# Decay logits of each head in 384 columns instead of 512, in a two-layer mLSTM and FoX trunk on one core

## The chip, the core and the metric

One core of a Trainium2 chip runs the whole program. Its engines work side by side and wait for each other by semaphores: TensorE (PE) multiplies matrices into PSUM, VectorE (DVE) and ScalarE (ACT) work on elements, GpSimd (POOL) does small jobs, SyncE (SP) issues most transfers from HBM. The metric is the device time of one execution in microseconds; the median of the runs of a kernel is compared.

## The reference

The input is 256 tokens of width 2048. Layer 0 mixes them by a stabilised mLSTM with 4 heads (queries and keys 256 wide, values 512), layer 1 by softmax attention with a forget gate (FoX, 16 heads of 128). Both are followed by a SwiGLU FFN of width 5632, and every norm is modulated by a condition vector (adaLN). Per head, the decayed scores of FoX are

```python
s = jnp.einsum('bhqd,bhkd->bhqk', qi, kf) * scale + cqi[..., None] - cum[..., None, :]
s = jnp.where(kpos[None, :] <= qpos[:, None], s, -jnp.inf)
p = jax.nn.softmax(s, axis=-1)
```

and those of the mLSTM

```python
D = b[..., :, None] - b[..., None, :] + lic[..., None, :]
D = jnp.where(causal, D, -jnp.inf)
m_t = jnp.maximum(inter_log, jnp.max(D, axis=-1))
w_intra = jnp.exp(D - m_t[..., None])
s = jnp.einsum('bhtd,bhsd->bhts', qc, kc) * w_intra
```

With two blocks of 128 tokens, the first block of queries sees only the first block of keys, the second sees both. So of 2 x 256 logits for each of 128 rows, 128 + 256 are used.

## The kernel before, in words

Nearly all the work is projections of the 256 tokens by weights that come from HBM in tiles of 1 MB. `fetch` (L252 to L255) loads such a tile into `rawp`, a pool of five buffers. `split` (L257) makes a high half (`hi`, a cast on ScalarE, L263) and a low half (`lo`, a subtraction on VectorE, L264) of each two rows of it, each from a pool of four buffers (`splitp`). `mm_t` (L287) then does three matmuls per piece: activation high by weight high (L290), high by low (L291), low by high (L292), 512 columns each. Their sums stand in six PSUM banks (`psum`, names mm); two more banks (`aux`) serve everything else: transposes, logits, scores.

The 1 MB tiles of the adaLN weights come through the same five buffers. `ada_tile` (L191) loads one on SyncE (L194) and multiplies and sums it on VectorE (L195, 128x2048). They are background work: a counter decides in which stage they are issued.

The mLSTM heads (`mlstm_head`) go in steps: `scores` (logits L678 and L683, exp L906, q·k L914, weighting L921), `flip` (transposes L893), `mix` (weights by values L945, squares L949, root L953, normalisation of both token blocks L957), `emit`. `emit` transposes the head into an aux bank (L970) and writes it scaled, as high half on ScalarE (L978) and low half on VectorE (L979), into a tile of `slots`; two such tiles a head. The steps of a head are laid between the matmuls of the stage that runs. Heads 2 and 3 fall into the beginning of the output projection (names mm_499, mm_500), which reads what `emit` wrote: its activations are first the slots of heads 0 and 1, then slot_493 and slot_495 of head 2. ScalarE's functions come from tables; exp, sigmoid (L800) and sqrt are in different ones, and a row ACT_TABLE_LOAD changes them.

`bridge` (L527) leads from one projection to the next through residual and norm. In its last part TensorE, VectorE and ScalarE follow the order in which the code is written: the last matmuls of the old projection for token block 0; on VectorE the gated residual (L429, L430); `rstd` (ScalarE's square and root, L457); `scale` (L474); transposes (L485); `high` (L495 on ScalarE, L497 on VectorE, four each); `low` (L510), the low half of the new activations; `begin` on TensorE, whose matmuls L552 and L553 need the high half and L556 the low half. Then the same again for token block 1. adaLN tiles that are still due are put between these rows when the program is built.

`split3` (L631) makes the decay sums of all heads of a layer into one tile `u3`: three bf16 parts at rows 0, 32 and 64. `logits` (L676) spreads the row of one head over 128 partitions by a matmul with a selecting column (`sel`, L678), and adds the causal mask of the diagonal blocks by another one (L683). In what order each engine takes its instructions is settled when the program is built, by a scheduler that models each instruction's time, except where the code fixes it.

Of the kernel before, what the change touches and what calls it, by code (L numbers as in the profile page):

```python
# [11 lines left out]
BF16 = mybir.dt.bfloat16  # L12
# [5 lines left out]
P = 128  # L18
T = 256
# [12 lines left out]
def kernel(  # L32
# [5 lines left out]
    nc = tc.nc  # L38
# [6 lines left out]
    att = ctx.enter_context(tc.tile_pool(name="att", bufs=1))  # L45
# [6 lines left out]
    def nm(s):  # L52
        n_name[0] += 1
        return f"{s}_{n_name[0]}"
# [21 lines left out]
    identb = const.tile([P, P], BF16, name="identb")  # L76
# [52 lines left out]
    for i, row in enumerate((crow, crow2)):  # L129
        for j in range(2):  # L130
            ps = bank()
# [497 lines left out]
        return u  # L629

    def split3(u, n, new):  # L631
        u3 = att.tile([96, T], BF16, tag="u3", name=nm("u3"), bufs=1)
        nc.gpsimd.memset(u3, 0.0)
        r = new()
        pp = new().bitcast(BF16)
        p, p2 = pp[:, :T], pp[:, T:]
        nc.vector.tensor_copy(p, u)
        nc.scalar.copy(u3[0:n, :], p)
        nc.vector.tensor_tensor(r, u, p, op=ALU.subtract)
        nc.vector.tensor_copy(p2, r)  # L640
        nc.scalar.copy(u3[32 : 32 + n, :], p2)
        nc.vector.tensor_tensor(r, r, p2, op=ALU.subtract)
        nc.scalar.copy(u3[64 : 64 + n, :], r)
        return u3

    def gate_weights(raw, pieces):
# [25 lines left out]
        nc.vector.tensor_tensor(g, ps[:n, :T], b, op=ALU.add)  # L672
        return g

    causal = ((0, P), (T, 2 * T))

    def logits(u3, h, ps, stop):
        nc.tensor.matmul(  # L678
            ps.rearrange("p (t s) -> p t s", t=2), sel[:, h : h + 1].to_broadcast([96, P]),
            u3[:, None, :].to_broadcast([96, 2, T]),  # L680
            start=True, stop=False, skip_group_check=True,
        )
        nc.tensor.matmul(  # L683
            ps.rearrange("p (b s) -> p b s", b=4)[:, 0::3, :], identb,
            mask[:, None, :].to_broadcast([P, 2, P]),
            start=False, stop=stop, skip_group_check=True,
        )
# [208 lines left out]
    def mlstm_head(hd, q, k):  # L896
        st = {}

        def scores():
            U = abank()  # L900
            logits(u3, hd, U, True)
            buf = slot()
            W = buf[:, : 3 * P]
            st["W"], st["WT"] = W, buf[:, 512 : 512 + 3 * P]
            for t in range(2):
                nc.scalar.activation(  # L906
                    W[:, slice(*packed[t])], U[:, slice(*causal[t])], AF.Exp,
                    bias=negT[:, t, hd : hd + 1],
                )
            S = abank()  # L910
            for t in range(2):
                n = P * (t + 1)
                for j in range(2):
                    nc.tensor.matmul(  # L914
                        S[:, T * t : T * t + n], q[:, j, t * P : (t + 1) * P], k[:, j, :n],
                        start=j == 0, stop=j == 1, skip_group_check=True,
                    )
            den = small([P, 2], "den", bufs=4)
            for t in range(2):
                wt = W[:, slice(*packed[t])]  # L920
                nc.vector.scalar_tensor_tensor(  # L921
                    out=wt, in0=S[:, slice(*causal[t])], scalar=1.0 / 16.0,
                    in1=wt, op0=ALU.mult, op1=ALU.mult, accum_out=den[:, t : t + 1],
                )
            r = small([P, 2], "r", bufs=4)
            nc.vector.scalar_tensor_tensor(
                out=r, in0=den, scalar=-1.0, in1=den, op0=ALU.mult, op1=ALU.max
            )
            nc.vector.tensor_tensor(r, r, em[:, :, hd], op=ALU.max)
            nc.vector.reciprocal(r, r)  # L930
            st["r"] = r
# [204 lines left out]
    def fox_head(hd, q, k):  # L1136
        st = {}

        def scores():
            S = abank()  # L1140
            logits(u3, hd, S, False)
            for t in range(2):
                n = P * (t + 1)
                nc.tensor.matmul(  # L1144
                    S[:, T * t : T * t + n], q[:, t * P : (t + 1) * P], k[:, :n],
                    start=False, stop=t == 1, skip_group_check=True,
                )
            mx = small([P, 2], "den", bufs=4)
            buf = slot()
            W = buf[:, : 3 * P]  # L1150
            st["W"], st["WT"] = W, buf[:, 512 : 512 + 3 * P]
            sm = small([P, 2], "r", bufs=4)
            for t in range(2):
                nc.vector.tensor_reduce(
                    out=mx[:, t : t + 1], in_=S[:, slice(*causal[t])], axis=AX.X, op=ALU.max,
                    negate=True,
                )
            for t in range(2):
                nc.scalar.activation(
                    W[:, slice(*packed[t])], S[:, slice(*causal[t])], AF.Exp,  # L1160
                    bias=mx[:, t : t + 1], accum_out=sm[:, t : t + 1],
                )
            nc.vector.reciprocal(sm, sm)
            for t in range(2):
                wt = W[:, slice(*packed[t])]
                nc.vector.tensor_scalar(wt, wt, sm[:, t : t + 1], None, op0=ALU.mult)
# [171 lines left out]
```

## Time and profile before

| | us |
|---|---|
| median of 3 runs | 2300.04 (2299.62 to 2301.35) |
| profiled execution | 2300.83 |
| its span | 2299.0 |
| TensorE busy | 2275.4 (99%) |
| VectorE busy | 1612.9 (70%) |
| ScalarE busy | 1122.8 (49%) |
| GpSimd busy | 15.6 (1%) |

The profiled execution is one run; its span is the time from the first to the last instruction in the profile, 1.8 us less than the run's own time. Busy times add up what an engine's instructions took. The granted clock of TensorE was 0.999 of full speed on average. The start-to-start distance of two matmuls tells what one costs in a row of them; its own duration is longer, since they overlap.

### The profile page before, as it was taken

The numbers are of one execution on the slowest core, as the hardware profiler recorded it, in microseconds if no ns is written. First come the engines' busy times: TensorE is split into PE (matmuls) and PEld (weight loads), VectorE is DVE, ScalarE is ACT, GpSimd is POOL, SyncE is SP. The second block draws the span as 40 slices with busy tenths as digits, with TensorE's granted clock in tenths as the row PEclk, the third lists the DMA queues.
The fourth block names the chain that finished last, engine by engine and source line by source line (L and its number), as shares of the span: only waits on it lengthen the run. The fifth ranks groups of instructions, "written<-read, shape, count | busy, mean of one in ns | idle before, by whom it ended". The sixth has DMA issues, their size and how long they took to land.

```text
span 2299.0 us, 26543 instructions
## 1 busy us (share of the span) xinstructions
PE 2275.4 (99%) x10376; PEld 1861.0 (81%) x10376; DVE 1612.9 (70%) x1829; ACT 1122.8 (49%) x1488; POOL 15.6 (1%) x40
## 2 busy tenths in 40 slices
PE   8999999999999999999999999999999999999998
PEld 4777878888888888888878888888888888888886
DVE  5998788878887878865687777777655554544554
ACT  3778664555543344444555444455444433444443
POOL 0000000000000000000000000000000000000000
PEclk9999999999999999999999999999999999999999
DMA  9998989798989889985667878775766555555552
GB/s 348 364 368 320 355 313 362 271 345 325 331 331 336 323 337 337 342 293 188 215 243 285 300 259 288 255 275 186 250 241 222 191 191 198 189 187 195 193 196 105
DMA packets 89090, 623.92 MB, mean 271 GB/s; under 512 B 10034, under 2 KB 10482, under 8 KB 14596
## 3 DMA queue, kind: packets, MB, share of 16 engines
q1 hardware_dynamic: 87552, 617.79, 74.3%
q0 software_dynamic: 1264, 4.29, 0.5%
q8 instruction: 81, 1.33, 0.2%
q14 instruction: 45, 0.37, 0.0%
q10 hardware_dynamic: 148, 0.14, 0.0%
HBM read 620.05 MB, written 2.13 MB: 271 GB/s over the span
## 4 chain that ended last, share of the span: by engine, by line
PE 88%; DVE 6%; DMA 3%; ACT 2%; issue 1%; SPq 0%; ACTq 0%; DVEq 0%
PE mm L292 25%; PE mm L291 25%; PE mm L290 25%; PE mm L273 5%; DVE ada L195 3%; PE mm L276 2%; DVE lo L264 2%; DMA ada<-in_ada_w_dram 2%; PE aux L347 1%; ACT hi L263 1%; DMA raw<-in_w_in_dram 1%; DMA slot<-in_w_in_dram 1%; PE aux L945 0%; PE aux L485 0%; PE aux L1144 0%
## 5 line engine op out<-in xcount | busy, mean ns | idle before, releaser
L264 DVE TENSOR_TENSOR lo<-raw,hi 128x1024 fp32r<-128x1024 f32 x764 | 926.9, 1223 | 556.8 <-ACT hi L263 556.2
L263 ACT CAST hi<-raw 128x1024 fp32r<-128x1024 f32 x764 | 797.1, 1053 | 920.3 <-PE mm L292 816.9
L291 PE MATMUL mm<-lo,hT 128*128 128x512 f32 x1840 | 718.3, 390 | 5.3 <-DVE lo L264 5.3
L290 PE MATMUL mm<-hi,hT 128*128 128x512 f32 x1840 | 719.3, 393 | 0.0
L292 PE MATMUL mm<-hi,hT 128*128 128x512 f32 x1840 | 718.1, 390 | 0.0
L195 DVE SCALAR_TENSOR_TENSOR ada<-ada,cs 128x2048 f32<-128x2048 f32 x192 | 438.9, 2286 | 49.2 <-DMA ada<-in_ada_w_dram 49.2
L291 PEld LDWEIGHTS mm<-lo,hT 128*128 128x128 f32 x1840 | 345.7, 188 | 80.1 <-DVE lo L264 10.2
L292 PEld LDWEIGHTS mm<-hi,hT 128*128 128x128 f32 x1840 | 345.4, 188 | 72.7 <-issue 0.5
L290 PEld LDWEIGHTS mm<-hi,hT 128*128 128x128 f32 x1840 | 345.3, 188 | 70.9 <-ACT hi L263 0.5
L290 PE MATMUL mm<-hi,slot 128*128 128x512 f32 x960 | 375.1, 391 | 0.2 <-ACT slot L978 0.2
L291 PE MATMUL mm<-lo,slot 128*128 128x512 f32 x960 | 374.4, 390 | 0.0
L292 PE MATMUL mm<-hi,slot 128*128 128x512 f32 x960 | 374.4, 391 | 0.0
L290 PEld LDWEIGHTS mm<-hi,slot 128*128 128x128 f32 x960 | 180.3, 188 | 37.7 <-ACT slot L978 0.8
L292 PEld LDWEIGHTS mm<-hi,slot 128*128 128x128 f32 x960 | 180.2, 188 | 37.6 <-issue 0.7
L291 PEld LDWEIGHTS mm<-lo,slot 128*128 128x128 f32 x960 | 180.2, 188 | 37.0
L273 PE MATMUL mm<-hT,hi 128*128 128x512 f32 x512 | 181.7, 402 | 0.6 <-DVE slot L359 0.6
L276 PE MATMUL mm<-hT,lo 128*128 128x256 f32 x512 | 138.3, 280 | 0.0
L273 PEld LDWEIGHTS mm<-hT,hi 128*128 128x128 f32 x512 | 94.4, 188 | 20.5 <-DVE slot L359 0.9
L276 PEld LDWEIGHTS mm<-hT,lo 128*128 128x128 f32 x512 | 96.6, 189 | 3.0
L800 ACT ACTIVATE slot<-mm 128x512 f32<-128x512 f32 x78 | 45.0, 593 | 33.9 <-PE mm L292 31.1
L435 ACT ACTIVATE t<-X 128x512 f32<-128x512 f32 x32 | 20.2, 631 | 39.2 <-DVE X L430 39.2
L1085 ACT ACTIVATE slot<-mm 128x512 f32<-128x512 f32 x44 | 25.4, 598 | 15.0 <-PE mm L292 13.8
(207 smaller groups left out, 980.5 us busy)
## 6 DMA issues: line engine op xcount, KB each, us to landing
ada<-in_ada_w_dram SPq DMA_DIRECT2D x192, 1024.0 KB, 6.5
raw<-in_gate_up_dram SPq DMA_DIRECT2D x176, 1024.0 KB, 4.9
raw<-in_down_dram SPq DMA_DIRECT2D x88, 1024.0 KB, 4.9
raw<-in_fox_in_dram SPq DMA_DIRECT2D x48, 1024.0 KB, 5.0
raw<-in_w_in_dram SPq DMA_DIRECT2D x44, 1024.0 KB, 7.3
raw<-in_w_out_dram SPq DMA_DIRECT2D x16, 1024.0 KB, 5.8
raw<-in_fox_out_dram SPq DMA_DIRECT2D x16, 1024.0 KB, 4.9
slot<-in_w_in_dram SPq DMA_DIRECT2D x16, 256.0 KB, 12.1
```

What stands on the lines that cost most here:

```text
L195: nc.vector.scalar_tensor_tensor(out=raw, in0=raw, scalar=1.0, in1=cs, op0=ALU.mult, op1=ALU.mult, accum_out=acc[layer][:, j : j + 1],)
L263: nc.scalar.copy(hi, raw[:, j : j + 2, :])
L264: nc.vector.tensor_tensor(lo, raw[:, j : j + 2, :], hi.bitcast(F32), op=ALU.subtract)
L273: nc.tensor.matmul(ps, hi, rhs, start=first, stop=last, skip_group_check=True)
L276: nc.tensor.matmul(ps[:, T:], lo, rhs[:, :T], start=False, stop=False, skip_group_check=True)
L290: nc.tensor.matmul(ps, a, hi, start=first, stop=False, skip_group_check=True)
L291: nc.tensor.matmul(ps, a, lo, start=False, stop=False, skip_group_check=True)
L292: nc.tensor.matmul(ps, b, hi, start=False, stop=last, skip_group_check=True)
L347: nc.tensor.transpose(ps[:, j * T + t * P : j * T + (t + 1) * P], src[:, t, (2 * i + j) * P : (2 * i + j + 1) * P], ident,)
L435: nc.scalar.activation(t512(), X[:, t, 512 * i : 512 * (i + 1)], AF.Square, accum_out=self.ss[:, t, i : i + 1],)
L800: nc.scalar.activation(SP[i][:, t, :], banks[t], func)
L1085: nc.scalar.activation(sg[:, t, :], banks[t], AF.Silu)
```

## The change

The causal pieces of the logits are put behind one another: the second block of queries, which sees all 256 tokens, in columns 0 to 255 of the bank, since the table now reads `causal = ((T, T + P), (0, T))`, so the first block's 128 columns stand at 256 to 383. `u3` gets 128 more columns that hold a copy of its first 128 (one more copy on ScalarE per layer, a wider memset on GpSimd). The selection matmul then writes 384 columns in one go instead of twice the 256; the mask matmul writes the two diagonal blocks, which are now neighbours, in columns 128 to 383; and the q·k matmuls of both kinds of head write where `causal` says. What reads the logits uses `causal` and follows.

```diff
-        u3 = att.tile([96, T], BF16, tag="u3", name=nm("u3"), bufs=1)
+        u3 = att.tile([96, T + P], BF16, tag="u3", name=nm("u3"), bufs=1)
         nc.gpsimd.memset(u3, 0.0)
...
-        nc.scalar.copy(u3[0:n, :], p)
+        nc.scalar.copy(u3[0:n, :T], p)
...
-        nc.scalar.copy(u3[32 : 32 + n, :], p2)
+        nc.scalar.copy(u3[32 : 32 + n, :T], p2)
...
-        nc.scalar.copy(u3[64 : 64 + n, :], r)
+        nc.scalar.copy(u3[64 : 64 + n, :T], r)
+        nc.scalar.copy(u3[:, T:], u3[:, :P])
         return u3
...
-    causal = ((0, P), (T, 2 * T))
+    causal = ((T, T + P), (0, T))

     def logits(u3, h, ps, stop):
         nc.tensor.matmul(
-            ps.rearrange("p (t s) -> p t s", t=2), sel[:, h : h + 1].to_broadcast([96, P]),
-            u3[:, None, :].to_broadcast([96, 2, T]),
+            ps[:, : T + P], sel[:, h : h + 1].to_broadcast([96, P]), u3,
             start=True, stop=False, skip_group_check=True,
         )
         nc.tensor.matmul(
-            ps.rearrange("p (b s) -> p b s", b=4)[:, 0::3, :], identb,
+            ps[:, P : T + P].rearrange("p (b s) -> p b s", b=2), identb,
             mask[:, None, :].to_broadcast([P, 2, P]),
...
-                        S[:, T * t : T * t + n], q[:, j, t * P : (t + 1) * P], k[:, j, :n],
+                        S[:, slice(*causal[t])], q[:, j, t * P : (t + 1) * P], k[:, j, :n],
...
-                    S[:, T * t : T * t + n], q[:, t * P : (t + 1) * P], k[:, :n],
+                    S[:, slice(*causal[t])], q[:, t * P : (t + 1) * P], k[:, :n],
```

With the new sizes the scheduler puts rows into another order in three stretches: where the mLSTM heads 2 and 3 meet the output projection, in the bridge to the first FFN, and by some exchanges in that FFN. In the FoX layer only the sizes change. Lines 645 to 681 stand one line lower in the changed kernel; from 682 on the numbers are the same in both. Of a name such as hi_532_2775 the middle number is the same in both kernels, and the last is higher by one in the changed one.

**ScalarE, head 2 into slot_493 and slot_495.** Before:

```order
L953 ACT_TABLE_LOAD
L953 ACTIVATE hrs_479_2530<-hsq_478_2529,eps_t_93 128x2
L263 CAST hi_525_2735<-raw_522_2729 128x1024
L402 COPY t512_483_2545<-aux_482_2543 16x128
L263 CAST hi_530_2771<-raw_529_2769 128x1024
L978 ACTIVATE slot_493_2590<-aux_494_2591,prm_115 128x256
L978 ACTIVATE slot_495_2600<-aux_496_2601,prm_115 128x256
L263 CAST hi_532_2775<-raw_529_2769 128x1024
L978 ACTIVATE slot_493_2590<-aux_494_2591,prm_115 128x256
L978 ACTIVATE slot_495_2600<-aux_496_2601,prm_115 128x256
```

Now:

```order
L263 CAST hi_525_2736<-raw_522_2730 128x1024
L953 ACT_TABLE_LOAD
L953 ACTIVATE hrs_479_2531<-hsq_478_2530,eps_t_93 128x2
L263 CAST hi_530_2772<-raw_529_2770 128x1024
L402 COPY t512_483_2546<-aux_482_2544 16x128
L263 CAST hi_532_2776<-raw_529_2770 128x1024
L978 ACTIVATE slot_493_2591<-aux_494_2592,prm_115 128x256
L978 ACTIVATE slot_495_2601<-aux_496_2602,prm_115 128x256
L978 ACTIVATE slot_493_2591<-aux_494_2592,prm_115 128x256
L978 ACTIVATE slot_495_2601<-aux_496_2602,prm_115 128x256
```

The root of head 2 (hrs_479) goes behind the cast of hi_525, and the cast of hi_532 ahead of the first two L978. A table load for the root stands in both; two more, not shown, stand ahead of these rows, where the exps of heads 2 and 3 now have a sigmoid between them (19 table loads in all before, 21 now).

**VectorE, the same stage.** Before:

```order
L957 SCALAR_TENSOR_TENSOR slot_477_2528<-aux_481_2534,hrs_479_2530,slot_104_541 128x512
L264 TENSOR_TENSOR lo_526_2736<-raw_522_2729,hi_525_2735 128x1024
L195 SCALAR_TENSOR_TENSOR ada_534_2803,acc0_124<-ada_534_2803,cs_144 128x2048
L264 TENSOR_TENSOR lo_531_2772<-raw_529_2769,hi_530_2771 128x1024
L979 SCALAR_TENSOR_TENSOR slot_493_2590<-aux_494_2591,prm_115,slot_493_2590 128x256
L979 SCALAR_TENSOR_TENSOR slot_495_2600<-aux_496_2601,prm_115,slot_495_2600 128x256
L264 TENSOR_TENSOR lo_533_2776<-raw_529_2769,hi_532_2775 128x1024
L979 SCALAR_TENSOR_TENSOR slot_493_2590<-aux_494_2591,prm_115,slot_493_2590 128x256
L979 SCALAR_TENSOR_TENSOR slot_495_2600<-aux_496_2601,prm_115,slot_495_2600 128x256
L195 SCALAR_TENSOR_TENSOR ada_546_2852,acc0_124<-ada_546_2852,cs_144 128x2048
```

Now:

```order
L957 SCALAR_TENSOR_TENSOR slot_477_2529<-aux_481_2535,hrs_479_2531,slot_104_541 128x512
L264 TENSOR_TENSOR lo_531_2773<-raw_529_2770,hi_530_2772 128x1024
L195 SCALAR_TENSOR_TENSOR ada_534_2804,acc0_124<-ada_534_2804,cs_144 128x2048
L264 TENSOR_TENSOR lo_533_2777<-raw_529_2770,hi_532_2776 128x1024
L979 SCALAR_TENSOR_TENSOR slot_493_2591<-aux_494_2592,prm_115,slot_493_2591 128x256
L979 SCALAR_TENSOR_TENSOR slot_495_2601<-aux_496_2602,prm_115,slot_495_2601 128x256
L195 SCALAR_TENSOR_TENSOR ada_546_2853,acc0_124<-ada_546_2853,cs_144 128x2048
L979 SCALAR_TENSOR_TENSOR slot_493_2591<-aux_494_2592,prm_115,slot_493_2591 128x256
L979 SCALAR_TENSOR_TENSOR slot_495_2601<-aux_496_2602,prm_115,slot_495_2601 128x256
```

The subtraction of lo_526 went ahead of this piece, that of lo_531 ahead of ada_534, that of lo_533 ahead of the first pair of L979, and ada_546 between the two pairs. On TensorE, fifteen matmuls of hi_513 and hi_515 stood between the transposes of head 2 (L970, aux_496) and the first matmul of hi_523 by slot_493; now there are two, and thirteen stand ahead of the transposes.

**VectorE, first half of the bridge and the beginning of the second.** Before:

```order
L429 TENSOR_TENSOR t512_639_3290<-mm_600_3143,slot_486_2550 128x512
L430 TENSOR_TENSOR X_129<-X_129,t512_639_3290 128x512
L457 RECIPROCAL rstd1_641_3316<-rstd1_641_3316 128x1
L474 TENSOR_SCALAR slot_642_3319<-X_129,rstd1_641_3316 128x512
L195 SCALAR_TENSOR_TENSOR ada_672_3526,acc0_124<-ada_672_3526,cs_144 128x2048
L497 TENSOR_SCALAR t512_645_3331<-aux_644_3326,mods0_122 128x128 x4
L510 TENSOR_TENSOR hT_134<-t512_645_3331,hT_134 128x4x128
L429 TENSOR_TENSOR t512_646_3356<-mm_601_3144,slot_486_2550 128x512
L430 TENSOR_TENSOR X_129<-X_129,t512_646_3356 128x512
L195 SCALAR_TENSOR_TENSOR ada_679_3566,acc0_124<-ada_679_3566,cs_144 128x2048
L457 RECIPROCAL rstd1_648_3361<-rstd1_648_3361 128x1
L474 TENSOR_SCALAR slot_649_3364<-X_129,rstd1_648_3361 128x512
```

Now:

```order
L429 TENSOR_TENSOR t512_639_3291<-mm_600_3144,slot_486_2551 128x512
L195 SCALAR_TENSOR_TENSOR ada_672_3527,acc0_124<-ada_672_3527,cs_144 128x2048
L430 TENSOR_TENSOR X_129<-X_129,t512_639_3291 128x512
L457 RECIPROCAL rstd1_641_3317<-rstd1_641_3317 128x1
L474 TENSOR_SCALAR slot_642_3320<-X_129,rstd1_641_3317 128x512
L497 TENSOR_SCALAR t512_645_3332<-aux_644_3327,mods0_122 128x128 x4
L195 SCALAR_TENSOR_TENSOR ada_679_3567,acc0_124<-ada_679_3567,cs_144 128x2048
L510 TENSOR_TENSOR hT_134<-t512_645_3332,hT_134 128x4x128
L429 TENSOR_TENSOR t512_646_3357<-mm_601_3145,slot_486_2551 128x512
L430 TENSOR_TENSOR X_129<-X_129,t512_646_3357 128x512
L457 RECIPROCAL rstd1_648_3362<-rstd1_648_3362 128x1
L474 TENSOR_SCALAR slot_649_3365<-X_129,rstd1_648_3362 128x512
```

ada_672 went from behind L474 to ahead of L430, and ada_679 from behind the second L430 to ahead of the first L510. In the second half, ada_686 now stands directly behind this piece, ahead of the four L497 and L510 of token block 1; before, those two followed with nothing between them. TensorE's rows of the bridge keep their order; on ScalarE some casts ahead of the first L429 changed places.

## Rows read from the trace of the kernel before

**Rows 1.** The page, busy us of each engine (share), and instructions.

```profile
PE 2275.4 (99%) x10376; PEld 1861.0 (81%) x10376; DVE 1612.9 (70%) x1829; ACT 1122.8 (49%) x1488; POOL 15.6 (1%) x40
```

**Rows 2.** TensorE's waits behind 445 us, the longest: total, times, longest us.

```profile
PE mm L556 <- DVE hT L510: 0.9, 1, 0.9
```

**Rows 3.** Timeline of TensorE, 276 to 279 us: start us, duration us, instruction.

```profile
276.57 0.39 PE L678 MATMUL aux<-u,sel 96*128 96x512 bf16 x1
276.80 0.27 PE L683 MATMUL aux<-mask,identb 128*128 128x256 bf16 x1
276.92 1.47 PE L914 MATMUL aux<-slot,slot 128*128 128x128 f32 x8
```

**Rows 4.** Timeline of ScalarE, 300 to 345 us.

```profile
324.53 1.28 ACT L906 ACT_TABLE_LOAD   x1
325.82 0.73 ACT L906 ACTIVATE slot<-aux,negT 128x128 f32<-128x128 f32 x2
...
341.80 1.06 ACT L263 CAST hi<-raw 128x1024 fp32r<-128x1024 f32 x1 [0.95 <-PE mm L292]
342.76 0.83 ACT L978 ACTIVATE slot<-aux,prm 128x256 fp32r<-128x256 f32 x2
```

**Rows 5.** Timeline of TensorE, 312 to 345 us; in brackets idle time, releaser.

```profile
337.24 1.09 PE L970 MATMUL aux<-ident,slot 128*128 128x128 f32 x8
338.09 0.48 PE L290 MATMUL mm<-hi,slot 128*128 128x512 f32 x1
...
343.28 0.50 PE L290 MATMUL mm<-hi,slot 128*128 128x512 f32 x1 [0.15 <-ACT slot L978]
...
344.08 0.40 PE L291 MATMUL mm<-lo,slot 128*128 128x512 f32 x1
344.66 0.67 PE L945 MATMUL aux<-slot,slot 128*128 128x512 f32 x1 [0.19 <-DVE slot L979]
```

**Rows 6.** Timeline of VectorE, 300 to 345 us.

```profile
342.89 1.23 DVE L264 TENSOR_TENSOR lo<-raw,hi 128x1024 fp32r<-128x1024 f32 x1 [0.45 <-ACT hi L263]
344.03 0.87 DVE L979 SCALAR_TENSOR_TENSOR slot<-aux,prm,slot 128x256 fp32r<-128x256 f32 x2
344.82 2.28 DVE L195 SCALAR_TENSOR_TENSOR ada<-ada,cs 128x2048 f32<-128x2048 f32 x1
```

**Rows 7.** Timeline of VectorE, 395 to 420 us.

```profile
417.18 0.69 DVE L429 TENSOR_TENSOR t<-mm,slot 128x512 f32<-128x512 f32 x1 [0.85 <-PE mm L292]
417.90 0.69 DVE L430 TENSOR_TENSOR X<-X,t 128x512 f32<-128x512 f32 x1
...
419.91 0.49 DVE L474 TENSOR_SCALAR slot<-X,rstd 128x512 f32<-128x512 f32 x1
```

**Rows 8.** Timeline of TensorE, 420 to 439 us.

```profile
421.74 1.03 PE L485 MATMUL aux<-ident,slot 128*128 128x128 f32 x8
...
425.12 1.10 PE L556 MATMUL mm<-slot,hT 128*128 128x512 f32 x4
...
429.17 1.09 PE L485 MATMUL aux<-ident,slot 128*128 128x128 f32 x8 [0.21 <-DVE slot L474]
...
432.52 1.20 PE L556 MATMUL mm<-slot,hT 128*128 128x512 f32 x4
```

**Rows 9.** Timeline of VectorE, 420 to 439 us.

```profile
422.82 1.36 DVE L497 TENSOR_SCALAR t<-aux,mods 128x128 f32<-128x128 f32 x4 [0.21 <-PE aux L485]
424.29 0.69 DVE L510 TENSOR_TENSOR hT<-t,hT 128x512 fp32r<-128x512 f32 x1
...
426.22 2.29 DVE L195 SCALAR_TENSOR_TENSOR ada<-ada,cs 128x2048 f32<-128x2048 f32 x1
```

**Rows 10.** Timeline of SyncE's DMA queue, 395 to 445 us.

```profile
428.54 0.33 SPq L194 DMA_DIRECT2D ada<-in_ada_w_dram  x1
```

**Rows 11.** DMA issues, 426 to 445 us: count, KB, us to landing.

```profile
ada<-in_ada_w_dram SPq DMA_DIRECT2D x2, 1024.0 KB, 5.1
```

**Rows 12.** The page, DMA issues, the same columns.

```profile
ada<-in_ada_w_dram SPq DMA_DIRECT2D x192, 1024.0 KB, 6.5
```

## The prediction, made before the changed kernel was run

> **What bounds the kernel now.** I read the page's busy times first: TensorE works for 2275.4 us of a span of 2299.0 us [rows 1]. So the kernel takes as long as TensorE's list of matmuls and whatever time TensorE stands still. The list of its waits shows how little that is: behind 445 us the longest is 0.9 us [rows 2]. Two kinds of edit can move the time: fewer columns for TensorE, and a new order on VectorE or ScalarE that makes TensorE wait. The change does both. The order in which each engine takes its instructions is fixed when the program is built, so a row that moved ahead of another there goes ahead of it on the chip, ready or not.
>
> The profiled execution took 2300.83 us, 0.79 us over the median of 2300.04 us. The sum is made on the profiled one and 0.79 us is taken off at the end. A difference of 0.2%, 4.6 us, is about what a measurement of this kernel can tell from none.
>
> **The columns: -1.1 us.** The selection matmul over 512 columns starts 0.23 us before the mask matmul, and that one, over 256 columns, 0.12 us before the next [rows 3]. Both are about 0.45 ns a column, so 128 columns fewer save 0.057 us, and 20 heads (4 in layer 0, 16 in layer 1) save 1.1 us. TensorE has no idle time there, so all of it counts. If the matmul's length did not follow its columns, it would be 0; that is the other bound. The q·k matmuls keep their sizes.
>
> The mask matmul now writes two neighbouring blocks instead of two that lie apart, and its row says that this is worth nothing: lying apart, it already takes the same time per column as the selection matmul beside it, which writes in one piece [rows 3]. The Trainium skill, PSUM — Partial Sum Buffer, section Specifications (TRN2), says that a non-contiguous access pattern slows matmuls significantly; by that the mask matmuls would get shorter too, by less than the 20 times 0.12 us that they take, and the sum would be up to 2.4 us lower. The row disagrees, and I go by the row.
>
> **The added copies: nothing.** Once per layer ScalarE copies 96x128 more and POOL clears half as many columns again. The nearest row is a cast of 128x1024 at 1.06 us [rows 4]; two copies are under 2.2 us of an engine that is on TensorE's path at few places, in a stretch where TensorE works on projections. If the projections did not cover them, both would cost their 2.2 us. I take 0.
>
> **The stage of the last two mLSTM heads, about 337 to 345 us: +3.2 us.** Three rows moved. On TensorE the transposes of head 2 (L970) had 15 projection matmuls behind them before the first matmul that reads the transposed head (slot_493); now 2. On ScalarE the cast of hi_532 stands ahead of the first scaling into slot_493 (L978) instead of behind it. On VectorE the scaling of ada_546 stands between the first and the second pair of L979.
>
> Count from the start p of the transposes. Before, it was 337.24 and the next matmul came 0.85 us later, at 338.09 [rows 5]. The second, and last, of the old matmuls thus starts at p+1.08, and TensorE is free at p+1.31. The cast of hi_532 takes the last free one of four split buffers, that of hi_515, which this matmul reads for 0.39 us: cast at p+1.5. From cast to L978 it is 0.96 us (341.80 to 342.76) [rows 4], from L978 to the matmul 0.52 us (342.76 to 343.28) [rows 4, 5]: p+2.98. **First wait 1.67 us.**
>
> Three matmuls on (p+3.78) the next wants the low half that L979 writes. From cast to subtraction is 1.09 us, subtraction 1.14 us, L979 0.4 us [rows 4, 6]: p+4.2 at the earliest. If VectorE is late, it has the subtraction of lo_531, ada_534 and the subtraction of lo_533 still to do when the transposes start, 1.14 + 2.28 + 1.14, and L979 is done at about p+5.0. **Second wait 0.4 to 1.2 us.** Seven matmuls on, 1.6 us, L945 wants the bank that the second L979 pair reads first. Ahead of that stand the rest of the first pair (0.4 us) and ada_546 (2.28 us), then 0.4 us of its own [rows 6]: 3.0 us after the first L979. **Third wait 1.4 us.** That is 3.5 to 4.3 us. Before, TensorE waited twice there itself: 344.08 to 344.66 is 0.35 us over the usual step of 0.23, and the other of 0.15 us idle is taken at 0.31 [rows 5]. Net 2.8 to 3.6; I take 3.2.
>
> TensorE itself comes to the transposes later, 13 matmuls by 0.23 is 3.0 us, and this is what covers the two extra table loads on ScalarE: 1.28 us each [rows 4], 2.6 us, which delay the normalisation that the transposes want. Without that cover they would cost up to 2.6 us.
>
> **The bridge to FFN 0, 417 to 433 us: +4.5 us.** This is a chain TensorE – VectorE – ScalarE – TensorE. First half: count from m, the start of L429, 417.18 [rows 7]. Now ada_672 (2.28 us) stands ahead of L430 instead of behind L474: L430 at m+2.9 instead of m+0.72. L474 follows 2.01 us after L430 as before (417.90 to 419.91) and takes 0.49 [rows 7], so the transposes can go at m+5.4; before, TensorE came to them at m+4.56 (421.74) [rows 8]. L497 comes 1.08 us after them (422.82) [rows 8, 9] at m+6.5; four of them 1.3 us; then ada_679, 2.28 us, now ahead of L510: L510 at m+10.1. L556 starts 0.83 us behind L510 (424.29 to 425.12) [rows 8, 9]: m+10.9. Before: 425.12, m+7.94, where TensorE's own work ended at the same moment, so there is no slack. **+3.0 us.**
>
> Second half: count from that L510, n (424.29). TensorE reaches the next transposes at n+4.67 (429.17 less the 0.21 us idle) [rows 8], L497 could start at n+5.75, but ada_686 now stands ahead of it. Its transfer is issued when the buffer of ada_679 has been read: before, that read ended at 426.22 + 2.29 and the transfer was issued at 428.54 [rows 9, 10]. Now the read ends where L510 starts, n. It lands 5.1 us later [rows 11], the scaling ends at n+7.4, L510 comes 1.47 us after L497 (422.82 to 424.29) at n+8.9, L556 at n+9.7. Before: 432.52, n+8.2 [rows 8]. **+1.5 us**; 0 if the transfer is quicker than 3.4 us, +2.9 with the page's median of 6.5 us [rows 12]. The bridge: 4.5, from 3.0 to 5.9.
>
> **Sum:** -1.1 + 3.2 + 4.5 = +6.6 us, 2307.4 for an execution like the profiled one, 2306.6 against the median. By its own bounds 2304.7 (-1.1 + 2.8 + 3.0) to 2309.5 (0 + 3.6 + 5.9).
>
> **Rivals.**
> *Only one place costs* (0.13): the wait in the head stage or that in the bridge is covered by work that I placed wrongly. 2302.1 with the head stage alone (-1.1 + 3.2), 2303.4 with the bridge alone (-1.1 + 4.5). For it: 0.4 to 1.7 us a piece are small. Against: TensorE had no slack at either place even before.
>
> *Not slower: the stock of ready matmuls covers the moved VectorE rows* (0.08): 2298.9, the columns alone. It decides at two points: the second L979 pair must end 1.4 us sooner after the transposes and the cast find a free buffer; and the bridge's ada tiles must be done before L429. Against it: L429 is released by TensorE's own last matmul (0.85 us idle before it) [rows 7], so VectorE cannot start sooner and the 2 times 2.28 us lie inside the chain. Nor can it be given back later: no later wait is over 0.9 us [rows 2].
>
> *The table switches cost more* (0.06): two more switches between exp, sigmoid and sqrt stand in ScalarE's list. The trace has 1.28 us for a load and the next activation 1.29 us after its start (324.53 to 325.82) [rows 4], so nothing behind the load. If each cost as much again, 2.6 us would lie beyond the cover of 3.0 us by 2.2 us and more rows of head 2 would be late: about 2309. The Trainium skill, ScalarE: Activation LUTs, section What ACT_TABLE_LOAD costs, puts a drain of about 1.38 us on top of each load, which is this rival; the trace shows none here.
>
> *The change does not do what it says* (0.03): the selection matmul is no shorter with fewer columns: 2307.7.
>
> *A gain beyond the bound* (0.04): the later TensorE lets transfers and casts run ahead for long enough to close most of the small idle times elsewhere; no row speaks for it.
>
> **How the numbers follow.** The forecast itself has 0.66. Forecast, dearer switches and columns without gain are all slower by over 0.2%: 0.75. One place only and no waits lie within 0.2%: 0.21. Faster: 0.04. The predicted time is the forecast's, 2306.6. The range goes from 2302.0, which takes in the one-place cases, to 2310.5, one us over the upper bound for part of the dearer switches; it leaves out the no-wait case and the gain, 0.12, and the far ends of the rest.
>
> **What would show it.** Right: the selection matmul's start-to-next time at 0.17 us instead of 0.23 in 20 places; in TensorE's waits two or three new entries between 335 and 355 us for L978 and L979, 3.5 us or more together; L556 about 10.9 us behind the first L429, and the wait at the second L556 named after L510; TensorE's busy time lower by about 1 us and the span longer by 6 to 7. Behind 450 us every stage as long as before, less 0.06 us a head. Wrong: no idle time of TensorE at L556, a wait list as short as before, or a difference that grows evenly over the span instead of in these two stages.

## The result, and the profile after

The changed kernel took 2304.51 us (median of 10 runs, 2302.03 to 2306.99) against 2299.32 us before (10 runs, 2296.27 to 2303.74). The ratio is 1.0024, with an interval of 1.0016 to 1.0033: slower by 3.7 to 7.6 us. A second set of runs of it (e6 below) gave 1.0029 (1.0019 to 1.0039). The forecast was 6.6 us slower.

The page of the profiled execution, in the same row as [rows 1]:

```profile
PE 2274.8 (99%) x10376; PEld 1861.0 (81%) x10376; DVE 1612.7 (70%) x1829; ACT 1125.1 (49%) x1492; POOL 15.8 (1%) x40
```

TensorE is busy for 0.6 us less than before, and the span of this execution is 2305.0 us against 2299.0, so the added time is idle time of TensorE. The 0.6 us themselves say little: a second trace of the kernel before has 2272.8 us of busy time, 2.6 us less than the first. TensorE's waits from 228 to 460 us, that is around the heads and the first bridge (what waited, for what: total us, times, longest):

```profile
PE mm L556 <- DVE hT L510: 3.5, 2, 1.7
PE mm L290 <- ACT slot L978: 1.5, 1, 1.5
PE aux L945 <- DVE slot L979: 1.2, 1, 1.2
PE mm L292 <- DVE slot L979: 1.2, 2, 0.8
PE aux L485 <- DVE slot L474: 0.7, 1, 0.7
```

That is 8.1 us of idle time. Before, this stretch had three waits of 0.2 us each, and [rows 5, 8] show all three. The two places of the forecast follow one by one.

**The heads.** TensorE's timeline in the changed kernel, where [rows 5] stood before (start us, duration, engine, line, operation; in brackets idle time and its releaser):

```profile
337.78 1.09 PE L970 MATMUL aux<-ident,slot 128*128 128x128 f32 x8
...
338.95 0.40 PE L292 MATMUL mm<-hi,slot 128*128 128x512 f32 x1
340.85 0.50 PE L290 MATMUL mm<-hi,slot 128*128 128x512 f32 x1 [1.51 <-ACT slot L978]
...
341.42 0.40 PE L290 MATMUL mm<-hi,slot 128*128 128x512 f32 x1
342.66 0.51 PE L292 MATMUL mm<-hi,slot 128*128 128x512 f32 x1 [0.84 <-DVE slot L979]
...
344.14 0.39 PE L291 MATMUL mm<-lo,slot 128*128 128x512 f32 x1
345.75 2.81 PE L945 MATMUL aux<-slot,slot 128*128 128x512 f32 x6 [1.22 <-DVE slot L979]
```

ScalarE and VectorE at the same place:

```profile
339.38 1.04 ACT L263 CAST hi<-raw 128x1024 fp32r<-128x1024 f32 x1 [1.65 <-PE mm L292]
340.33 0.83 ACT L978 ACTIVATE slot<-aux,prm 128x256 fp32r<-128x256 f32 x2
```
```profile
338.78 2.29 DVE L195 SCALAR_TENSOR_TENSOR ada<-ada,cs 128x2048 f32<-128x2048 f32 x1
...
342.13 0.87 DVE L979 SCALAR_TENSOR_TENSOR slot<-aux,prm,slot 128x256 fp32r<-128x256 f32 x2
342.91 2.28 DVE L195 SCALAR_TENSOR_TENSOR ada<-ada,cs 128x2048 f32<-128x2048 f32 x1
...
345.12 0.87 DVE L979 SCALAR_TENSOR_TENSOR slot<-aux,prm,slot 128x256 fp32r<-128x256 f32 x2
```

The transposes start at 337.78, so p of the prediction is 337.78. The last old matmul is at p+1.17, the first by slot_493 at p+3.07 (forecast 2.98): 1.90 us where 0.23 is the usual step, a wait of 1.67. From 341.42 to 342.66 it is 1.24, a wait of 1.01; from 344.14 to 345.75 it is 1.61, a wait of 1.38. Together 4.06 us, less the 0.66 us that the kernel before lost here.

The cast of hi_532 is released by the last old matmul and starts at p+1.60; the first L978 follows it by 0.95 us. ada_534 ends where the subtraction of lo_533 starts, 1.14 us ahead of the first pair of L979, and ada_546 fills the time from that pair to the second. The second entry of L979 in the list, 0.33 us at 358.70, belongs to head 3 and was not forecast.

**The bridge.** VectorE, where [rows 7, 9] stood before:

```profile
418.88 0.69 DVE L429 TENSOR_TENSOR t<-mm,slot 128x512 f32<-128x512 f32 x1 [2.92 <-PE mm L292]
419.49 2.28 DVE L195 SCALAR_TENSOR_TENSOR ada<-ada,cs 128x2048 f32<-128x2048 f32 x1
...
421.70 0.69 DVE L430 TENSOR_TENSOR X<-X,t 128x512 f32<-128x512 f32 x1
...
426.71 2.29 DVE L195 SCALAR_TENSOR_TENSOR ada<-ada,cs 128x2048 f32<-128x2048 f32 x1
...
428.92 0.69 DVE L510 TENSOR_TENSOR hT<-t,hT 128x512 fp32r<-128x512 f32 x1
...
434.00 2.29 DVE L195 SCALAR_TENSOR_TENSOR ada<-ada,cs 128x2048 f32<-128x2048 f32 x1 [1.26 <-DMA ada<-in_ada_w_dram]
...
436.22 1.36 DVE L497 TENSOR_SCALAR t<-aux,mods 128x128 f32<-128x128 f32 x4
```

and TensorE, where [rows 8] stood:

```profile
424.33 1.06 PE L485 MATMUL aux<-ident,slot 128*128 128x128 f32 x8 [0.73 <-DVE slot L474]
...
429.67 1.20 PE L556 MATMUL mm<-slot,hT 128*128 128x512 f32 x4 [1.75 <-DVE hT L510]
...
438.43 1.19 PE L556 MATMUL mm<-slot,hT 128*128 128x512 f32 x4 [1.72 <-DVE hT L510]
```

Count from L429 at 418.88. The scaling of ada_672 stands ahead of L430, which starts at 421.70; TensorE waits 0.73 us for the input of the transposes. Then ada_679 (426.71) stands ahead of L510 (428.92), and L556 starts 10.79 us behind L429 (forecast 10.9; before 7.94). From that L510 it goes on: the transfer of ada_686 is issued when ada_679 has been read:

```profile
429.04 0.33 SPq L194 DMA_DIRECT2D ada<-in_ada_w_dram  x1
```

It lands late (VectorE idles 1.26 us for it), L497 starts behind the tile at 436.22, and the second L556 comes 9.51 us behind L510 (forecast 9.7; before 8.23).

**The columns.** A head of layer 1 in the changed kernel, where [rows 3] show one of layer 0 before:

```profile
1285.15 0.34 PE L679 MATMUL aux<-u,sel 96*128 96x384 bf16 x1
1285.32 0.27 PE L683 MATMUL aux<-mask,identb 128*128 128x256 bf16 x1
1285.43 0.82 PE L1144 MATMUL aux<-slot,slot 128*128 128x128 f32 x4
```

The selection matmul is followed after 0.17 us instead of 0.23. The mask matmul, which now writes in one piece, lasts 0.27 us and is followed after 0.11, as before. The 19 other heads have the same first step, 0.16 to 0.18 us in place of 0.22 to 0.23.

**The ledger.** Five marks cut every trace: the first selection matmul of layer 0 (A), the first L429 of the first bridge (B), the end of that bridge (C, the first projection matmul behind its last transposes), and the first and last selection matmul of layer 1 (D and E). The starts of these rows, subtracted:

| us | span to A | A to B | B to C | D to E |
|---|---|---|---|---|
| before | 276.6 | 140.6 | 19.9 | 194.6 |
| before, second trace (e11) | 273.0 | 140.6 | 19.9 | 194.8 |
| changed | 274.4 | 144.4 | 24.1 | 194.6 |
| changed, second trace (e6) | 272.3 | 144.0 | 24.1 | 193.8 |

The heads cost 3.4 to 3.8 us, the bridge 4.2 us. The 0.8 us of columns in layer 1 are there in the second trace; in the first, a wait of 0.3 us and some small steps took them up. Up to A both kernels have the same instructions in the same order, but for the one copy and the wider memset, yet the four executions differ by 4.2 us there. C to D, not in the table, is 842.5 and 841.2 us before and 842.2 and 840.8 in the changed kernel: it differs by as much from trace to trace of one kernel as the forecast has in its columns. So spans of single executions are not to be compared, but A to B and B to C are steady to some tenths.

### The profile page after: what moved, and what is told of

Same layout as the page of the kernel before. It is cut to its first block, busy times and chain, and to the rows that moved or that the text cites. A ratio compares the mean times of both kernels' runs of the same rounds, so it can differ in the third digit from the quotient of the medians.

```text
span 2305.0 us, 26543 instructions
## 1 busy us (share of the span) xinstructions
PE 2274.8 (99%) x10376; PEld 1861.0 (81%) x10376; DVE 1612.7 (70%) x1829; ACT 1125.1 (49%) x1492; POOL 15.8 (1%) x40
## 4 chain that ended last, share of the span: by engine, by line
PE 86%; DVE 6%; DMA 4%; ACT 2%; issue 1%; SPq 0%; ACTq 0%; DVEq 0%
PE mm L292 25%; PE mm L291 24%; PE mm L290 24%; PE mm L273 5%; DVE ada L195 3%; DMA ada<-in_ada_w_dram 3%; PE mm L276 2%; DVE lo L264 2%; PE aux L347 1%; ACT hi L263 1%; DMA slot<-in_w_in_dram 1%; PE aux L485 0%; PE mm L786 0%; PE aux L1144 0%; PE mm L556 0%
## 5 line engine op out<-in xcount | busy, mean ns | idle before, releaser
L264 DVE TENSOR_TENSOR lo<-raw,hi 128x1024 fp32r<-128x1024 f32 x764 | 927.4, 1223 | 560.0 <-ACT hi L263 557.9
L291 PE MATMUL mm<-lo,hT 128*128 128x512 f32 x1840 | 718.3, 390 | 4.1 <-DVE lo L264 4.1
L290 PE MATMUL mm<-hi,hT 128*128 128x512 f32 x1840 | 719.2, 393 | 0.0
L292 PE MATMUL mm<-hi,hT 128*128 128x512 f32 x1840 | 718.0, 390 | 0.0
L291 PEld LDWEIGHTS mm<-lo,hT 128*128 128x128 f32 x1840 | 345.7, 188 | 78.7 <-DVE lo L264 8.3
L292 PEld LDWEIGHTS mm<-hi,hT 128*128 128x128 f32 x1840 | 345.4, 188 | 72.5 <-issue 0.5
L290 PEld LDWEIGHTS mm<-hi,hT 128*128 128x128 f32 x1840 | 345.4, 188 | 70.2 <-ACT hi L263 0.2
L290 PE MATMUL mm<-hi,slot 128*128 128x512 f32 x960 | 375.0, 391 | 1.5 <-ACT slot L978 1.5
L292 PE MATMUL mm<-hi,slot 128*128 128x512 f32 x960 | 374.7, 391 | 1.2 <-DVE slot L979 1.2
L291 PE MATMUL mm<-lo,slot 128*128 128x512 f32 x960 | 374.2, 390 | 0.0
L292 PEld LDWEIGHTS mm<-hi,slot 128*128 128x128 f32 x960 | 180.2, 188 | 39.6 <-DVE slot L979 2.2
L290 PEld LDWEIGHTS mm<-hi,slot 128*128 128x128 f32 x960 | 180.3, 188 | 39.3 <-ACT slot L978 2.2
L291 PEld LDWEIGHTS mm<-lo,slot 128*128 128x128 f32 x960 | 180.3, 188 | 37.1
```

Of the source, the lines that this page charges most:

```text
L264: nc.vector.tensor_tensor(lo, raw[:, j : j + 2, :], hi.bitcast(F32), op=ALU.subtract)
L290: nc.tensor.matmul(ps, a, hi, start=first, stop=False, skip_group_check=True)
L291: nc.tensor.matmul(ps, a, lo, start=False, stop=False, skip_group_check=True)
L292: nc.tensor.matmul(ps, b, hi, start=False, stop=last, skip_group_check=True)
```

## The experiments

In all of them the ratio is against runs of the kernel before on the same chip. Line numbers of the variants are shifted; the text names the lines of the changed kernel.

**e1, e7: the columns in layer 1 alone.** Layer 0 goes back to 512 columns with a second `logits` and a second table, on the wider `u3`:

```diff
-            logits(u3, hd, U, True)
+            logits_wide(u3, hd, U, True)
```

> 384 columns in the 16 heads of layer 1 alone; layer 0 keeps 512, and with it every row of layer 0 stands as in the kernel before. Theory (the loss is the new order in layer 0, the columns are a small gain): 16 x 0.055 = 0.9 us faster than the kernel before, no wait of TensorE at L978, L979 or L510 between 330 and 440 us. Rival (the loss, or part of it, comes from the wider u3, its copies, or from the FoX stage): 1 to 5 us slower than the kernel before, with longer distances between the landmarks of the FoX stage.

> e1_fox_only once more, for its time. Theory: the heads of layer 1 take 193.7 us from their first to their last selection matmul (194.6 before), 0.9 us less, as in e1; the wait of 1.6 us at L485 in the bridge behind layer 1's projection, which the one execution of e1 had, is chance and changes. Over both runs 0.9 us faster than the kernel before. Rival (TensorE, 0.9 us earlier, only waits as much longer for the ada tile in that bridge): the wait at L485 is there again with over 0.8 us, and the time is that of the kernel before.

Measured: 1.0005 (0.9996 to 1.0013) and 0.9996 (0.9987 to 1.0005), so no difference that the runs can tell, and the loss of the changed kernel is gone. The 0.9 us that were expected are neither confirmed nor excluded by these times. In the traces D to E takes 193.7 us both times, 0.9 us less than before, as expected, and from 228 to 460 us there are only the three waits of 0.2 us. e1 lost the gain again in the bridge behind layer 1, at an ada tile that stands ahead of L429 there. VectorE and TensorE in e1:

```profile
1549.96 2.29 DVE L195 SCALAR_TENSOR_TENSOR ada<-ada,cs 128x2048 f32<-128x2048 f32 x1 [3.89 <-DMA ada<-in_ada_w_dram]
```
```profile
1555.54 1.06 PE L485 MATMUL aux<-ident,slot 128*128 128x128 f32 x8 [1.61 <-DVE slot L474]
```

The transfers of this stretch, median us to landing, in e1 and then in e7:

```profile
ada<-in_ada_w_dram SPq DMA_DIRECT2D x1, 1024.0 KB, 6.7
```
```profile
ada<-in_ada_w_dram SPq DMA_DIRECT2D x1, 1024.0 KB, 5.6
```

Where the tile landed in 5.6 us TensorE did not wait at L485; where it took 6.7, it waited 1.6 us. Neither trace of the kernel before waits there. The first trace of the changed kernel and those of e2, e3 and e12 wait 0.4 to 1.4 us, its second (e6) not at all. This is the scatter in which 0.9 us are lost, and it confirms neither rival: A to B is 140.7 us in e7 with the wider `u3`, both runs are as fast as the kernel before with the copies in them, and the gain is not always handed back. In layer 1 not only the sizes change: two of VectorE's ada tiles (ada_1833 and ada_1882) stand one row later than before. TensorE waits nowhere in these heads in either trace.

**e2: the columns in layer 0 alone.** The same the other way round.

> 384 columns in the 4 heads of layer 0 alone; layer 1 keeps 512. Layer 0 stands in the order of the changed kernel. Theory: the whole loss is here, +3.4 us at the heads and +4.2 us in the bridge less 0.2 us of columns: 7.4 us slower than the kernel before, 0.9 us slower than the changed kernel; L556 10.8 us behind the first L429 of the bridge. Rival (FoX stage shares in the loss): 4 us slower than before or less.

Measured: 1.0036 (1.0024 to 1.0048), 5.5 to 11 us slower. The waits between 228 and 460 us are those of the changed kernel, and L556 comes 10.79 us behind the first L429; D to E, with 512 columns, was 196.0 us in this execution, 1.2 us of it a wait that the kernel before does not have. Four heads with fewer columns, worth 0.2 us, carry the loss.

**e3: the bridge in its old order, within the changed kernel.** The ada tiles get an edge, a dependency that only the scheduler sees, which keeps them behind a row of VectorE in the order:

```diff
+        if anchors:
+            behind(ins, anchors.pop(0))
...
+        if len(bridged) == 0:
+            anchors.extend(held)
```

> The changed kernel, with ada_672, ada_679 and ada_686 held behind L474, the second L430 and the second L510, as the kernel before has them; from the bridge on all rows stand as before. Theory: the bridge's 4.2 us go, the three waits in the stage of the heads stay (1.5, 0.8 and 1.2 us idle): 2.3 us slower than the kernel before (3.4 less 1.1). Rival (waits in the bridge are only moved, and come back later in the FFN): no faster than the changed kernel, 5 to 6 us slower than before.

Measured: 1.0011 (1.0002 to 1.0020), 2.5 us slower than before; expected were 2.3. A to B is 144.2 us, B to C 19.9 us. Nothing came back in the FFN: C to D is 842.6 us, against 842.5 in the first trace of the kernel before.

**e4: the bridge in its new order, within the kernel before.** The three tiles are issued inside the bridge by hand, between the rows where the changed kernel has them; the weights that SyncE loads between them are fetched at the same places, so that its queue keeps its order:

```diff
             nc.vector.tensor_tensor(m, ps, self.G[i], op=ALU.mult)
+            if between:
+                between.pop()()
             nc.vector.tensor_tensor(cols, cols, m, op=ALU.add)
...
+                prefetch(w2, 4, heads[1])
+                extra()
             norm.low(0, 0)
```

> The kernel before with its 512 columns, and the three ada tiles put in the bridge where the changed kernel has them (the transfers on SyncE keep their order). Theory: L556 10.8 us behind the first L429 instead of 7.9, the second L556 9.5 us behind the first L510 instead of 8.2: 4.2 us slower than the kernel before, no new wait at the heads. Rival (it is the size of the logits that costs, not the order): as the kernel before, within 1 us.

Measured: 1.0029 (1.0017 to 1.0040), 3.9 to 9.2 us slower, with logits of 512 columns; the 4.2 us that were expected lie at the low end of that. A to B is 140.7 us as before, B to C 24.3, 4.4 more than before. TensorE in this bridge (L575 is L556 here, L516 is L510):

```profile
424.80 1.21 PE L575 MATMUL mm<-slot,hT 128*128 128x512 f32 x4 [1.75 <-DVE hT L516]
...
433.78 1.19 PE L575 MATMUL mm<-slot,hT 128*128 128x512 f32 x4 [1.90 <-DVE hT L516]
```

L429 was at 414.01, so L556 came 10.79 us behind it, to the hundredth as in the changed kernel. With e3 this shows that the bridge's loss is the order and nothing else.

**e5: ada_546 behind both pairs of L979** (the bridge held as in e3):

```diff
+        if n_name[0] == 546:
+            behind(ins, last_low[2])
```

> e3_bridge_old with one more ada tile held: ada_546 behind both pairs of L979 instead of between them. Theory (the third wait of the heads' stage is this tile): the wait of TensorE at L945 after L979 goes (1.2 us idle, 1.4 us from start to start), the other two stay at 1.5 and 0.9 us; about 1 us slower than the kernel before. Rival (L945 is held by something else, such as the scalar engine's L978): the wait stays over 0.8 us, 2.3 us slower than before.

Measured: 1.0005 (0.9996 to 1.0013), 1.1 us over the kernel before where about 1 was expected, though the runs cannot tell it from none. The waits from 228 to 460 us in e5 (L304 is L290, L1000 is L978, L306 is L292, L1001 is L979):

```profile
PE mm L304 <- ACT slot L1000: 1.5, 1, 1.5
PE mm L306 <- DVE slot L1001: 0.9, 1, 0.9
```

The wait at L945 is gone and the other two stand. A to B is 142.4 us, 1.8 less than in e3: the third wait was that tile. The wait itself was 1.4 us; the edge also moved other rows (L945 now stands three matmuls earlier), and to which of them the other 0.4 us belong is not shown.

**e12: the cast of hi_532 behind the first L978, on top of e5:**

```diff
+        if n_name[0] == 533:
+            behind(cast, first_high[2])
```

> e5_ada_behind_l979 with the cast of hi_532 held behind the first two L978 (the scheduler then puts the first two L979 ahead of the subtraction of lo_533 too). Theory (the first wait is that cast): the wait at L978 falls from 1.5 us to under 0.3 us, and the wait at L979 grows from 0.9 us to about 1.4 us, since ada_534 is still ahead of it on VectorE and ends about 3.4 us after the transposes start; about 0.8 us faster than e5. Rival (the first wait comes from the transposes): 1.5 us stay.

Measured: 1.0014 (1.0004 to 1.0023), not faster than e5 but some 2 us slower by the two ratios, whose intervals overlap; A to B is 144.7 us against 142.4. TensorE (L309 is L292, L1006 is L979, L308 is L291, L281 is L264):

```profile
340.08 0.50 PE L309 MATMUL mm<-hi,slot 128*128 128x512 f32 x1 [1.51 <-DVE slot L1006]
...
350.31 0.50 PE L308 MATMUL mm<-lo,slot 128*128 128x512 f32 x1 [1.74 <-DVE lo L281]
...
357.25 0.74 PE L309 MATMUL mm<-hi,slot 128*128 128x512 f32 x2 [0.56 <-DVE slot L1006]
```

The first row is as expected: no wait at L978, and 1.5 us at L979. So the first wait was the cast. But with the new edge the scheduler put ada_552 ahead of the subtraction of lo_543 and other rows elsewhere, and two waits that e5 does not have, 1.74 and 0.56 us, took more than the edge gave. The theory of the first wait holds, the forecast of the time failed: one edge moves more than one row.

**e6: the changed kernel again.**

> The changed kernel once more, unchanged, for a second trace. Theory (what differs between single executions lies in waits for transfers, the new order costs the same each time): from the first selection matmul of layer 0 to the first of layer 1 again 1010.7 us (1003.0 in the kernel before), with the same waits at L978, L979, L945 and L510 within 0.2 us; the stretch ahead of it (274.4 us in the first trace, 276.6 in the kernel before, the same instructions) and the one behind the heads of layer 1 differ by up to 2 us from the first trace. 5 to 6 us slower than before. Rival (the waits are themselves chance): other waits, by more than 1 us in sum.

Measured: 1.0029 (1.0019 to 1.0039), A to B and B to C as in the table above. The expectation missed twice. A to D, which was to be 1010.7 us, is 1008.9; 0.5 us of the difference lie between A and C, and most of the rest is shorter waits behind C (0.3 us for 0.8 in the FFN, none for 0.5 at L556 of the second bridge). And the wait at L945 is not in its list, which has 6.4 us where the first trace has 8.1. By its own sign, other waits by more than 1 us in sum, the rival would hold; but A to B and B to C are within half a microsecond of the first trace, so the cost is not chance. The last section says where the wait went.

**e11: the kernel before again.**

> The kernel before, unchanged, for a second trace. Theory: 1003 us from the first selection matmul of layer 0 to that of layer 1 within 1 us, 140.6 us of it to the first L429 of the first bridge, and 19.9 us from there to the end of the bridge, both within 0.1 us; 194.6 us in the heads of layer 1. The stretch ahead of the first selection matmul (276.6 us in the first trace) is shorter, 272 to 275 us as in the other kernels, whose instructions there are the same. Rival (the other kernels are faster there by their making): again 276 to 277 us.

Its marks are in the table. The stretch ahead of A was chance. A to D is 1.3 us shorter than in the first trace, just over what was expected; 0.9 of it is the wait at L556 of the second bridge [rows 2], which is not there in this trace.

**e8, e9, e10: the ada tiles held behind the second and third bridge too.** The same edge, in the kernel of e1 (e8 and, once more, e9) and in the kernel before (e10):

```diff
+        if len(bridged) == 1:
+            anchors.extend([held[-1], held[-1]])
+        if len(bridged) == 2:
+            anchors.append(held[-1])
```

> e1_fox_only with the ada tiles of the second and third bridge (one ahead of L429 and one ahead of L497; one ahead of L429) held behind the second L510 of their bridge. Theory (an ada tile inside a bridge lies on the chain VectorE - TensorE and costs what it is late): the waits at L556 in the second bridge (0.4 to 0.9 us) and at L485 in the third (0 to 1.6 us) go; 1.5 to 3 us faster than the kernel before. Rival (the tiles hold their buffers longer, and weights come later): new waits behind the bridges at L290 or L291, no faster than before.

> e8_held once more, for its time. Theory: again 1.5 to 3 us faster than the kernel before, no wait of TensorE inside the second and third bridge, the heads of layer 1 at 193.7 us. Rival (e8 was chance): within 1 us of the kernel before.

> The kernel before, with its 512 columns, and the ada tiles of the second and third bridge held as in e8. Theory: what e8 gains is 0.9 us of columns (194.6 against 193.7 us in the heads of layer 1) and the rest of the two bridges: 1 to 2 us faster than the kernel before. Rival (the columns give nothing in time): as fast as e8.

Measured: 0.9990 (0.9981 to 0.9999) and 0.9988 (0.9979 to 0.9997): 2.3 and 2.8 us faster than the kernel before, and some 8 us faster than the changed one, twice. From 1100 to 1600 us, with both bridges in it, TensorE waits nowhere in either trace; D to E is 193.7 and 193.8 us. The kernel before with the same edges gave 0.9996 (0.9987 to 1.0004), less than was expected of it. Its trace has waits of 1.0, 1.0 and 0.5 us between 460 and 1270 us, outside the bridges, but it is of a run of 2299.8 us where the median is 2296.9, so it does not say why. So e8 is a version that is faster than both, by 0.1% than the kernel before, with the columns where they do not disturb the order and no ada tile inside the two later bridges. How its 2.5 us divide between the two, these runs cannot tell.

## Why the prediction was right

*What bounds the kernel* held: the time moved with TensorE's waits, and a little with its columns.

*The columns, -1.1:* 0.17 us to the next matmul in place of 0.23, as worked out, in all the heads: 20 times 0.054 us, 1.1 us. The other sign that was named for it, a busy time of TensorE lower by about 1 us, cannot be read: two traces of the kernel before differ by 2.6 us in it. What the step did not see is that 0.9 us are no more than one late transfer, so that a single execution need not show them.

*The added copies, nothing:* up to A, with the copy of layer 0 in it, the changed kernel took 274.4 and 272.3 us, the kernel before 276.6 and 273.0, and C to D, with that of layer 1, differs from trace to trace as it does in the kernel before. Nothing is seen of the 2.2 us, though a few tenths would be lost in that scatter.

*The mask matmul:* in one piece it takes what it took in two [rows 3]. The Trainium skill, PSUM — Partial Sum Buffer, section Specifications (TRN2), would have it shorter; this trace does not bear that out for two blocks of 128 columns with a gap between them.

*The heads, +3.2:* waits of 1.67, 1.01 and 1.38 us where 1.67, 0.4 to 1.2 and 1.4 were forecast. The middle one came out near the upper end, the case of the late VectorE: its subtraction of lo_531, ada_534 and the subtraction of lo_533 stood back to back up to L979. That is read from the trace; no run took this wait away by itself, as e5 and e12 did with the other two. The two extra table loads were covered as forecast: TensorE waits for nothing from A to the transposes, which came 2.67 us later than before, counted from A, where 13 matmuls of 0.23 are 3.0 us. Little of the cover was left, since the normalisation that the transposes want ended at 337.73, 0.05 us ahead of their start. ScalarE at these loads:

```profile
320.72 1.28 ACT L906 ACT_TABLE_LOAD   x1
322.01 0.73 ACT L906 ACTIVATE slot<-aux,negT 128x128 f32<-128x128 f32 x2
322.76 1.28 ACT L800 ACT_TABLE_LOAD   x1
324.06 0.60 ACT L800 ACTIVATE slot<-mm 128x512 f32<-128x512 f32 x1
```

The activations start 1.29 and 1.30 us behind the start of their loads, and the second load directly behind the two activations ahead of it, so the rival of dearer switches found nothing. The drain that the Trainium skill, ScalarE: Activation LUTs, section What ACT_TABLE_LOAD costs, puts on top of each load does not show in these rows.

*The bridge, +4.5:* 4.2, of which 2.85 in the first half (forecast 3.0) and 1.3 in the second (1.5). The second half hung on how soon a transfer lands; with this order B to C is 24.0 to 24.3 us in four traces (both of the changed kernel, e2, e4), so here it was not luck.

*The rivals:* "only one place costs" fell, since e3 and e4 show each place alone. "The stock of ready matmuls covers it" fell too. It would have needed VectorE to run ahead, and L429 is released by TensorE itself, here as in [rows 7]. The selection matmul that does not get shorter fell with its 0.17 us, and no trace shows a gain beyond the bound.

Against the sum of 6.6 us the two sets of runs gave 5.2 and 6.7 us between their medians, each with an interval of about 2 us to either side, so they can tell smaller differences than the 4.6 us that the prediction took for the limit. The ledger behind A, 3.6 and 4.2 less 0.8, gives 7.0. In it the heads came out somewhat above their term and the bridge somewhat below, and the two errors cancel in part.

## What to carry to other kernels

A smaller instruction is also a new input to the scheduler: compare the order of every engine before and after, and count what each moved row delays, before counting the saving. A row of background work on VectorE (here 2.3 us of scaling) is cheap while other engines have work, but not inside a chain that goes from engine to engine: three such rows cost 4.2 us in one bridge, some four times what the columns saved. An edge can hold them behind the chain; it moves other rows too, so look at the whole order again after each.

## What was not expected of the hardware

In e6 and e3 the wait at L945 is missing, and the place still takes as long. The granted clock says why. Busy time and clock in e6 by stretches (us, then busy time and count of PE, PEld, DVE, ACT and POOL; then the granted clock of TensorE, and what the DMA engines did):

```profile
338.70:340.50 1.80, 0.96 (x3) 0.49 (x3) 1.80 (x5) 0.38 (x2) 0.00 (x0) 0.89 0.96 300
340.50:342.00 1.50, 1.44 (x3) 1.16 (x4) 1.50 (x3) 0.86 (x2) 0.64 (x2) 0.50 0.88 344
342.00:343.60 1.60, 1.60 (x5) 0.99 (x3) 1.60 (x4) 0.00 (x0) 0.45 (x1) 0.53 1.01 379
343.60:346.00 2.40, 2.40 (x8) 1.19 (x7) 1.18 (x3) 0.78 (x2) 0.00 (x0) 1.00 0.96 386
```

and its timeline:

```profile
338.76 0.50 PE L290 MATMUL mm<-hi,slot 128*128 128x512 f32 x1 [1.51 <-ACT slot L978]
...
340.56 0.80 PE L292 MATMUL mm<-hi,slot 128*128 128x512 f32 x1 [0.83 <-DVE slot L979]
341.15 0.63 PE L291 MATMUL mm<-lo,slot 128*128 128x512 f32 x1
341.58 0.63 PE L292 MATMUL mm<-hi,slot 128*128 128x512 f32 x1
...
343.65 2.81 PE L945 MATMUL aux<-slot,slot 128*128 128x512 f32 x6
```

TensorE idled 1.51 us and, three matmuls on, 0.83 us; in the second wait its granted clock fell from 1.00 to 0.50, that is from 2.4 to 1.2 GHz, for some 3 us, and its matmuls then came every 0.43 us instead of 0.23. L945 started 7.96 us behind the transposes (7.99 in e3), as in the first trace (7.97), where the clock stayed at 1.00: the slow matmuls only filled the time that TensorE would have waited for L979. In e2 and e5 too the first two waits were as long and the clock stayed at 1.00, so what decides is not shown. A short list of waits in a trace thus need not mean that a place costs less; the distance between two landmarks tells.
